# Requests for raw weights placed with the low that frees their buffer, v's weight sums requested with the last low, and another order of products in the latent opening

## The chip, the core and the metric

The kernel is one program on one core of a Trainium2 chip. Five engines run their own instruction streams: TensorE (PE in the profile; its weight loads are PEld), VectorE (DVE), ScalarE (ACT), GpSimd (POOL) and SyncE (SP, which here only issues transfers). The metric is device time in microseconds of one execution; lower is better. Values are the median of several runs.

## What is computed

Two layers over 512 latent and 256 context tokens of width 1024, float32. Each layer is a half-step SwiGLU FFN, a token mixer and a second half-step FFN, each with its input modulated by shift and scale, its output gated, and closed by a layer norm. Layer 0 mixes with a chunked gMLP, layer 1 with attention. Only the latent tokens are returned, so the last FFN runs over the latent tokens alone.

```python
def swiglu(h, w_in, w_out):
    g, u = jnp.split(h @ w_in, 2, axis=-1)
    return (jax.nn.silu(g) * u) @ w_out

def ffn_sublayer(x, shift, scale, gate, w_in, w_out, ln_g, ln_b):
    y = swiglu(modulate(x, shift, scale), w_in, w_out)
    return layer_norm(ALPHA * x + 0.5 * gate * y, ln_g, ln_b)

def gmlp_mix(h, w_in, sgu_g, sgu_b, w_s, b_s, w_out):
    u, v = jnp.split(jax.nn.gelu(h @ w_in, approximate=False), 2, axis=-1)
    v = layer_norm(v, sgu_g, sgu_b)
    ...
    return (u * v.reshape(b_, t_, GMLP_HALF)) @ w_out
```

## The kernel before

**Weights.** All weights come from HBM in pieces of 128x512 float32, 256 KB, called raws. `weight_order` writes out by hand the one order in which the whole kernel needs them. `load_raw` requests the next of that list on SP's queue as long as fewer than six raw buffers are out; `drop(n)` says that n buffers are given back and so requests n more; `take` hands over the oldest raw. SP's stream is pinned to program order, and a request there waits at the head of the queue until the last reader of its buffer is done.

**Units.** PE multiplies in a reduced float32 format, so a weight is used as a high part and a low part. `unit_of` makes a unit (w, eight buffers) of a raw or of a sum: ACT casts the high part (`hi`), and DVE subtracts to give the low part, the low. `split_later` (L175) issues the cast at once and puts the low on a list, `lows`; `flush` (L180) issues the lows. Each `slot`, the work between two groups of matmuls, begins with a flush, and then `pump` makes the next units, up to eight ahead of PE. So a low is issued one slot after its cast, unless `weights` needs it earlier.

**Strassen products.** The in-projections use a variant of Strassen's scheme: of four weight quarters (g1, g2, u1, u2) and four quarters of the activations, seven products are formed. `units` (L326) makes the seven units of a tile, with sums of raws on DVE: L348 and L351 make the first sums, L359 subtracts u1 from g1 in place, L367 makes the last. The units of u1 and u2 are split from the raw itself, so their raw buffer is free when their low has been made. Where a unit is a sum in a buffer of its own, the raws are free when that sum has been made.

**gmlp_v** (L1481) forms v, the second half of the gMLP's in-projection, in three pairs of 512 columns. For its sums of u1 and u2, `load_sums` (L429) loads the one raw into a buffer (acc, of which there are four) from SP's queue and lets a transfer of POOL's queue add the other to it on the way. `units_of_pair` (L437) subtracts a raw from the sum (`held`, on DVE), and later splits the sum itself: the lows of these four units (`s1`) are the last readers of acc. `load_sums` is called at the start of the stage, after the step T1 of the first pair, and after T1 of the second.

**The gMLP loop** (`gmlp`, L1623) then forms u in 12 pairs of 128 columns; in each it fetches pieces of v on SP's queue and fetches modulation weights (mraw), also on SP's queue, which DVE reduces into an accumulator.

**The latent opening.** The last FFN is `ffn_latent` (L1421). It starts while the layer norm ahead of it still runs: its first ten products are `open_pair(p, half)` in the order of `OPEN_LAT`, where p is a pair of column blocks and half is the part of the input that it multiplies. The first part of the activations (`comb`) is ready earlier than the second; between products, PE also transposes normalised rows, which ACT copies out (`pieces`, z). Its remaining weights are made by `units_of_tiles` (L385), and `out_proj_latent` follows. The weights of `OPEN_LAT` are requested in the same order (L229).

The steps of the prediction touch: `drop` and `take` (L308 to L312), `split_later`, `unit_of`, `units`, `units_of_tiles`, `load_sums`, `units_of_pair`, `gmlp_v` and `OPEN_LAT` (L64).

Of the kernel before, what the change touches and what calls it, by code (L numbers as in the profile page):

```python
# [7 lines left out]
F32 = mybir.dt.float32  # L8
F32R = mybir.dt.float32r
AF = mybir.ActivationFunctionType  # L10
ALU = mybir.AluOpType
# [49 lines left out]
KEPT_MIX, READ_BACK_MIX = 2, 10  # L61
KEPT_LAT, READ_BACK_LAT = 6, 9
OPENED_PAIRS = 5
OPEN_LAT = [(0, 0), (1, 0), (0, 1), (2, 0), (1, 1), (3, 0), (2, 1), (4, 0), (3, 1), (4, 1)]  # L64

PARTS = (0, 0), (0, 1), (1, 0)

# [31 lines left out]
class Backbone:  # L99
# [72 lines left out]
        self.dve.tensor_tensor(lo, src, hi.bitcast(F32), ALU.subtract)  # L172
        return i.ins

    def split_later(self, hi, lo, src, key=None):  # L175

        self.act.copy(hi, src)  # L177
        self.lows.append((key, lambda: self.dve.tensor_tensor(lo, src, hi.bitcast(F32), ALU.subtract)))  # L178

    def flush(self):  # L180
        lows, self.lows = self.lows, []
# [30 lines left out]
    def weight_order(self):  # L212
# [6 lines left out]
        def ffn(l, s, strassen=True, kernel_start=False):  # L219
# [3 lines left out]
            def cut(o, f, half):  # L223
                return wi[:, 4 * half : 4 * half + 4, o + f * P : o + f * P + P]

            start = FIRST_OPEN + SECOND_OPEN if kernel_start else OPEN
            if not strassen:
                two = lambda o, p, half: [cut(o, f, half) for f in (2 * p, 2 * p + 1)]
                jobs.append(("u", [s for p, half in OPEN_LAT for s in two(0, p, half)]))  # L229
                for p in range(FF // 2):  # L230
# [76 lines left out]

    def take(self):  # L308
        self.load_raw()
        return self.wraw.pop(0)  # L310

    def drop(self, n):  # L312
# [3 lines left out]
    def sums(self):  # L316
        return self.main.tile([P, 512], F32, tag="sums", bufs=2, name="sums")

    def unit_of(self, src):
        w = self.main.tile([P, 2, 512], F32R, tag="w", bufs=W_BUFS, name="w")  # L320
        self.split_later(w[:, 0], w[:, 1], src, w)
        if not self.slots:
            self.flush()
        return w

    def units(self, jobs):  # L326
        dve, w = self.dve, None
        for kind, srcs in jobs:
            if kind == "u":
                for _ in srcs:  # L330
                    w = self.unit_of(self.take())
                    self.drop(1)
                    yield w
                continue
            if kind in "vw":
                yield from self.units_of_pair(kind == "w")
                continue
            if kind in "RS":
                yield from self.units_of_tiles(kind == "R")
                continue  # L340
            g1 = self.take()
            if kind == "s":
                yield self.unit_of(g1)
            u1, u2 = self.take(), self.take()
            if any(key is w for key, _ in self.lows):
                self.flush()
            s1, s2 = self.sums(), self.sums()
            dve.tensor_tensor(s1, u1, u2, ALU.add)  # L348
            if kind == "s":
                yield self.unit_of(s1)  # L350
            dve.tensor_tensor(s2, s1, g1, ALU.subtract)  # L351
            second = self.unit_of(s2)
            yield second
            if kind == "r":
                yield self.unit_of(s1)
            else:
                g2 = self.take()
                yield self.unit_of(g2)
            dve.tensor_tensor(u1, g1, u1, ALU.subtract)  # L359
            w = self.unit_of(u1)  # L360
            self.drop(2)
            yield w
            if kind == "r":
                g2 = self.take()
            if any(key is second for key, _ in self.lows):
                self.flush()
            dve.tensor_tensor(s2, g2, s2, ALU.subtract)  # L367
            w = self.unit_of(s2)
            self.drop(1)
            yield w  # L370
            w = self.unit_of(u2)
            self.drop(1)
            yield w

    def load_tile_sums(self):

# [8 lines left out]
    def units_of_tiles(self, opened):  # L385

        sub = lambda out, a, b: self.dve.tensor_tensor(out, a, b, ALU.subtract)
        self.load_tile_sums()
        g1 = [self.take() for _ in range(2)]
        if not opened:  # L390
            for g in g1:
                yield self.unit_of(g)
        s1 = [self.tile_sums.pop(0) for _ in range(2)]
        if not opened:
            for s in s1:
                yield self.unit_of(s)
        s2, second = [], []
        for g, s in zip(g1, s1):
            s2.append(self.sums())
            sub(s2[-1], s, g)  # L400
            second.append(self.unit_of(s2[-1]))
            yield second[-1]
        if opened:
            for s in s1:
                yield self.unit_of(s)
        else:
            g2 = [self.take() for _ in range(2)]
            for g in g2:
                yield self.unit_of(g)
        for g in g1:  # L410
            u1 = self.take()
            sub(u1, g, u1)
            w = self.unit_of(u1)
            self.drop(2)
            yield w
        for x in range(2):
            g = self.take() if opened else g2[x]
            if any(key is second[x] for key, _ in self.lows):
                self.flush()
            sub(s2[x], g, s2[x])  # L420
            w = self.unit_of(s2[x])
            self.drop(1)
            yield w
        for _ in range(2):
            w = self.unit_of(self.take())
            self.drop(1)
            yield w

    def load_sums(self):  # L429

        self.u_sums = [self.acc() for _ in range(4)]
        u1, u2 = self.pair_sums.pop(0)
        for k in range(4):
            self.sp.dma_start(self.u_sums[k], u1[k])
            self.pool.dma_start(self.u_sums[k], u2[k], accum_op=ALU.add)

    def units_of_pair(self, first):  # L437

        def of_raw():
            for _ in range(4):  # L440
                w = self.unit_of(self.take())
                self.drop(1)
                yield w

        held = self.main.tile([P, 4, 512], F32, tag="gate", bufs=1, name="held")
        s1, units = self.u_sums, []
        for k in range(4):
            g1 = self.take()
            self.dve.tensor_tensor(held[:, k], s1[k], g1, ALU.subtract)
            units.append(self.unit_of(held[:, k]))  # L450
            self.drop(1)
            yield units[k]
        if first:
            yield from of_raw()
        else:
            for k in range(4):
                yield self.unit_of(s1[k])
        for k in range(4):
            g1, u1 = self.take(), self.take()
            self.dve.tensor_tensor(u1, g1, u1, ALU.subtract)  # L460
            w = self.unit_of(u1)
            self.drop(2)
            yield w
        if first:
            for k in range(4):
                yield self.unit_of(s1[k])
            yield from of_raw()
        for k in range(4):
            g2 = self.take()
            if any(key is units[k] for key, _ in self.lows):  # L470
                self.flush()
            self.dve.tensor_tensor(held[:, k], g2, held[:, k], ALU.subtract)
            w = self.unit_of(held[:, k])
            self.drop(1)
            yield w
        if not first:
            yield from of_raw()
# [943 lines left out]
    def ffn_latent(self, l, i, nblocks, end, prev):  # L1421
# [3 lines left out]
        self.combining = self.combine_latent()  # L1425
        for n, (p, half) in enumerate(OPEN_LAT):
            self.open_pair(p, half, self.seed if n == len(OPEN_LAT) - 2 else None)
        acts = Acts(self, FF, LAT, KEPT_LAT, READ_BACK_LAT, f"act{l}{i}_")
# [52 lines left out]
    def gmlp_v(self, room, spill, vst):  # L1481
# [61 lines left out]
        def zs():  # L1543
            return [self.zplace() for _ in range(HALF)]

        def ms():
            return [
                self.main.tile([P, 512], F32, tag="mraw", bufs=MRAW_BUFS, name="p5") for _ in range(HALF)
            ]

        def keep(p):
            return lambda t, ps: act.copy(p[t], ps)
# [10 lines left out]
        def kept_and_seeded(p5, u2):  # L1563

            def evacuate(t, ps):
                act.copy(p5[t], ps)
                act.copy(ps, u2[t])

            return evacuate
# [19 lines left out]
        u2 = zs()  # L1589
# [3 lines left out]
        step(1, "T3", True, keep(u3))  # L1593
        p5 = ms()
        step(0, "T1", False, kept_and_seeded(p5, u2))
        self.load_sums()

        def fourth(t, ps):
            out(1, t, ps)
# [6 lines left out]
        for x, a, seed in ((1, 2, p2), (0, 4, None)):  # L1606
            y = 1 - x
            u2 = zs()
            step(x, "T2", True, keep(u2))
            p5 = ms()  # L1610
            step(y, "T1", False, kept_and_seeded(p5, u2))
            if seed:
                self.load_sums()
            step(x, "T3", True, lambda t, ps, a=a, p5=p5: summed(a + 1, HALF + t, ps, p5[t]))
            step(y, "B22", True, both(a, p5, seed))
            step(x, "T4", True, lambda t, ps, a=a: out(a + 1, t, ps))
# [938 lines left out]
```

## Time and profile before

| | |
|---|---|
| median of 3 runs | 2761.05 us (2759.3 to 2762.8) |
| the profiled execution | 2765.46 us, its span 2763.5 us |
| mean granted clock of TensorE | 0.996 |
| PE busy | 2713.8 us, 98% of the span |
| DVE, ACT, POOL busy | 2135.2, 1375.4, 675.7 us |
| SP's queue (q1) | 343.00 MB, 40.5% of the 16 DMA engines' time |
| POOL's queue (q0) | 122.42 MB, 15.5% |

The stages that the change touches most lie at 559 to 739 us (gmlp_v), 740 to 954 (the gMLP loop) and 2400 to 2439 (the latent opening). In a timeline, each row gives start, duration, engine, line, operation, what it writes and reads, and how many there were in a row; in brackets stands the idle time of that engine ahead of it and what ended the idle time. L94 is the line of the helper that pins an instruction, so instructions are told apart by their tiles. "SPq" and "POOLq" stand for transfers issued on the queues of SP and POOL.

### The profile page before, as it was taken

The numbers are of one execution on the slowest core, as the hardware profiler recorded it, in microseconds if no ns is written. First come the engines' busy times: TensorE is split into PE (matmuls) and PEld (weight loads), VectorE is DVE, ScalarE is ACT, GpSimd is POOL, SyncE is SP. The second block draws the span as 40 slices with busy tenths as digits, with TensorE's granted clock in tenths as the row PEclk, the third lists the DMA queues.
The fourth block names the chain that finished last, engine by engine and source line by source line (L and its number), as shares of the span: only waits on it lengthen the run. The fifth ranks groups of instructions, "written<-read, shape, count | busy, mean of one in ns | idle before, by whom it ended". The sixth has DMA issues, their size and how long they took to land.

```text
span 2763.5 us, 42802 instructions
## 1 busy us (share of the span) xinstructions
PE 2713.8 (98%) x14930; PEld 2479.1 (90%) x14930; DVE 2135.2 (77%) x3724; ACT 1375.4 (50%) x2755; POOL 675.7 (24%) x829
## 2 busy tenths in 40 slices
PE   7999999999999999999999999999999999999998
PEld 5999987888899988899998889999988888899987
DVE  6878878576779977687888658788786598788865
ACT  6644433375666632564444237444432666665532
POOL 1003245312113344100324130024253121112221
PEclk9999999999999999999999999999999999999999
DMA  7445466367665684444446534454595424489772
GB/s 236 134 141 143 145 217 223 110 198 229 196 200 182 198 274 127 133 146 149 138 144 220 175 108 137 141 155 138 170 309 168 144 78 75 135 212 237 196 230 87
DMA packets 442896, 468.15 MB, mean 169 GB/s; under 512 B 30840, under 2 KB 323128, under 8 KB 442680
## 3 DMA queue, kind: packets, MB, share of 16 engines
q1 hardware_dynamic: 393592, 343.00, 40.5%
q0 software_dynamic: 49088, 122.42, 15.5%
q8 instruction: 117, 1.92, 0.3%
q14 instruction: 99, 0.81, 0.1%
HBM read 401.75 MB, written 65.77 MB: 169 GB/s over the span
## 4 chain that ended last, share of the span: by engine, by line
PE 74%; DVE 7%; issue 6%; ACT 5%; DMA 4%; POOL 3%; SPq 0%; DVEq 0%; ACTq 0%; POOLq 0%
PE ps L94 74%; POOL acc L544 2%; DVE w L94 2%; DMA raw<-in_ffn_w_in_dram 1%; ACT w L94 1%; PE pp L94 1%; ACT h L765 1%; DMA raw<-in_w_mod_dram 1%; DVE q L94 1%; ACT z L2453 0%; ACT w L177 0%; DVE z L94 0%; DMA acc<-in_gmlp_w_in_dram 0%; DMA q<-act 0%; POOL rs L208 0%
## 5 line engine op out<-in xcount | busy, mean ns | idle before, releaser
L94 PE MATMUL ps<-comb,w 128*128 128x384 f32 (+1 forms) x8400 | 1379.3, 324 | 14.0 <-ACT pieces L94 3.7
L94 PEld LDWEIGHTS ps<-comb,w 128*128 128x128 f32 x8400 | 1360.2, 189 | 21.3 <-ACT pieces L94 4.3
L94 PE MATMUL ps<-w,acts 128*128 128x512 f32 (+1 forms) x3792 | 861.6, 388 | 1.6 <-DVE q L94 0.8
L94 PEld LDWEIGHTS ps<-w,acts 128*128 128x128 f32 x3792 | 706.9, 188 | 148.5 <-ACT acts L94 1.2
L94 DVE TENSOR_TENSOR w<-raw,w 128x512 fp32r<-128x512 f32 x651 | 453.2, 703 | 258.8 <-ACT w L94 256.4
L94 ACT CAST w<-raw 128x512 fp32r<-128x512 f32 x651 | 399.4, 622 | 496.3 <-PE ps L94 395.1
L544 POOL PARTITION_ALL_REDUCE acc<-acc x224 | 294.9, 1388 | 260.2 <-DVE acc L94 231.8
L94 DVE SCALAR_TENSOR_TENSOR acc<-mraw,cs,acc 128x512 f32<-128x512 f32 x392 | 285.2, 761 | 16.1 <-DMA mraw<-in_w_mod_dram 15.7
L94 ACT COPY q<-ps 128x384 f32<-128x384 f32 (+1 forms) x248 | 122.1, 495 | 257.7 <-PE ps L94 257.0
L94 POOL DMA_DIRECT2D act<-stage x92 | 59.4, 716 | 779.8 <-DVE stage L94 733.7
L94 DVE TENSOR_TENSOR w<-sums,w 128x512 fp32r<-128x512 f32 x278 | 191.4, 697 | 52.6 <-ACT w L94 51.5
L94 POOL DMA_DIRECT2D q<-act x240 | 135.9, 621 | 338.1 <-DVE acts L94 197.3
L94 ACT CAST w<-sums 128x512 fp32r<-128x512 f32 x278 | 171.6, 621 | 62.2 <-DVE sums L94 30.7
L94 DVE TENSOR_TENSOR acts<-q,acts 128x384 fp32r<-128x384 f32 (+2 forms) x278 | 152.3, 587 | 32.5 <-ACT acts L94 32.5
L94 PE MATMUL ps<-w,comb 128*128 128x512 f32 x756 | 173.8, 390 | 3.3 <-ACT ps L94 2.9
L94 PEld LDWEIGHTS ps<-w,comb 128*128 128x128 f32 x756 | 141.3, 188 | 34.4 <-ACT ps L94 3.8
L94 ACT CAST acts<-q 128x384 fp32r<-128x384 f32 (+2 forms) x278 | 132.0, 512 | 72.1 <-DMA q<-act 54.3
L208 POOL TENSOR_TENSOR rs<-ve,mhalf 128x1 f32<-128x1 f32 (+3 forms) x47 | 38.2, 812 | 264.6 <-DVE ve L205 161.1
L94 ACT ACTIVATE q<-q 128x384 f32<-128x384 f32 (+1 forms) x94 | 51.3, 553 | 87.2 <-DVE q L94 87.2
L348 DVE TENSOR_TENSOR sums<-raw 128x512 f32<-128x512 f32 x78 | 55.1, 707 | 41.0 <-DMA raw<-in_gmlp_w_in_dram 25.4
L94 PE MATMUL ps<-w,h 128*128 128x512 f32 x336 | 78.2, 391 | 0.0
L178 DVE TENSOR_TENSOR w<-raw,w 128x512 fp32r<-128x512 f32 x93 | 61.7, 687 | 18.8 <-ACT w L177 18.4
(201 smaller groups left out, 2459.4 us busy)
## 6 DMA issues: line engine op xcount, KB each, us to landing
raw<-in_ffn_w_in_dram SPq DMA_DIRECT2D x420, 256.0 KB, 3.4
mraw<-in_w_mod_dram SPq DMA_DIRECT2D x256, 256.0 KB, 3.0
raw<-in_ffn_w_out_dram SPq DMA_DIRECT2D x176, 256.0 KB, 2.9
q<-act POOLq DMA_DIRECT2D x224, 192.0 KB, 4.1
raw<-in_gmlp_w_in_dram SPq DMA_DIRECT2D x132, 256.0 KB, 3.3
act<-stage POOLq DMA_DIRECT2D x76, 384.0 KB, 3.2
zhat<-z POOLq DMA_DIRECT2D x26, 512.0 KB, 3.0
raw<-in_gmlp_w_out_dram SPq DMA_DIRECT2D x48, 256.0 KB, 4.6
```

The source lines that it names most:

```text
L94: return self.tc.keep_in_program_order(f(*args, **kwargs))
L178: self.lows.append((key, lambda: self.dve.tensor_tensor(lo, src, hi.bitcast(F32), ALU.subtract)))
L208: self.last_rstd = self.nc.gpsimd.tensor_tensor(rs, ve, self.mhalf[:, 0:1].to_broadcast([P, n]), ALU.pow).ins
L348: dve.tensor_tensor(s1, u1, u2, ALU.add)
L544: nc.gpsimd.partition_all_reduce(part, part, P, bass_isa.ReduceOp.add)
L765: self.act.activation(h32[:, kk], ps[:, s], AF.Identity, bias=bi, scale=sc)
```

## The change

Three things. (1) The request that takes the place of a raw enters SP's queue when the low that reads this raw is issued, not when its cast is issued: `drop` becomes an argument of `unit_of` and is done in the function that issues the low. Where a unit of u1 gave two raws back, the one that only its subtraction reads is given back at once, and the other with the low. `take` issues the waiting lows if no raw is requested. (2) `load_sums` of v is called by the last low of `s1` (through the argument `then`), no longer after T1; the call at the start of the stage stays. (3) `OPEN_LAT` has (2, 0) third and (0, 1) fourth. What is computed is the same.

```diff
-OPEN_LAT = [(0, 0), (1, 0), (0, 1), (2, 0), (1, 1), (3, 0), (2, 1), (4, 0), (3, 1), (4, 1)]
+OPEN_LAT = [(0, 0), (1, 0), (2, 0), (0, 1), (1, 1), (3, 0), (2, 1), (4, 0), (3, 1), (4, 1)]

-    def split_later(self, hi, lo, src, key=None):
+    def split_later(self, hi, lo, src, key=None, drop=0, then=None):
         self.act.copy(hi, src)
-        self.lows.append((key, lambda: self.dve.tensor_tensor(lo, src, hi.bitcast(F32), ALU.subtract)))
+
+        def low():
+            self.dve.tensor_tensor(lo, src, hi.bitcast(F32), ALU.subtract)
+            if drop:
+                self.drop(drop)
+            if then:
+                then()
+
+        self.lows.append((key, low))

     def take(self):
         self.load_raw()
+        if not self.wraw:
+            self.flush()
         return self.wraw.pop(0)

# units: a raw that is split itself ("u" jobs; the same in units_of_tiles and units_of_pair)
-                    w = self.unit_of(self.take())
-                    self.drop(1)
-                    yield w
+                    yield self.unit_of(self.take(), 1)

# units: g1 less u1 (the same in units_of_tiles and units_of_pair)
             dve.tensor_tensor(u1, g1, u1, ALU.subtract)
-            w = self.unit_of(u1)
-            self.drop(2)
-            yield w
+            self.drop(1)
+            yield self.unit_of(u1, 1)

# units: u2
-            w = self.unit_of(u2)
-            self.drop(1)
-            yield w
+            yield self.unit_of(u2, 1)

     def load_sums(self):
+        if not self.pair_sums:
+            return
...
# units_of_pair, both places
             for k in range(4):
-                yield self.unit_of(s1[k])
+                yield self.unit_of(s1[k], 0, self.load_sums if k == 3 else None)

# gmlp_v
         step(0, "T1", False, kept_and_seeded(p5, u2))
-        self.load_sums()
...
             step(y, "T1", False, kept_and_seeded(p5, u2))
-            if seed:
-                self.load_sums()
```

More of the change, by code (lines that the diff above doesn't have):

```diff
@@ L317, in sums, with unit_of @@
         return self.main.tile([P, 512], F32, tag="sums", bufs=2, name="sums")
-    def unit_of(self, src):
+    def unit_of(self, src, drop=0, then=None):
         w = self.main.tile([P, 2, 512], F32R, tag="w", bufs=W_BUFS, name="w")
-        self.split_later(w[:, 0], w[:, 1], src, w)
+        self.split_later(w[:, 0], w[:, 1], src, w, drop, then)
         if not self.slots:
@@ L412, in units_of_tiles @@
             sub(u1, g, u1)
-            w = self.unit_of(u1)
-            self.drop(2)
-            yield w
+            self.drop(1)
+            yield self.unit_of(u1, 1)
         for x in range(2):
@@ L424, in units_of_tiles @@
         for _ in range(2):
-            w = self.unit_of(self.take())
-            self.drop(1)
-            yield w
+            yield self.unit_of(self.take(), 1)
     def load_sums(self):
+        if not self.pair_sums:
+            return
         self.u_sums = [self.acc() for _ in range(4)]
@@ L440, in of_raw @@
             for _ in range(4):
-                w = self.unit_of(self.take())
-                self.drop(1)
-                yield w
+                yield self.unit_of(self.take(), 1)
         held = self.main.tile([P, 4, 512], F32, tag="gate", bufs=1, name="held")
@@ L460, in units_of_pair @@
             self.dve.tensor_tensor(u1, g1, u1, ALU.subtract)
-            w = self.unit_of(u1)
-            self.drop(2)
-            yield w
+            self.drop(1)
+            yield self.unit_of(u1, 1)
         if first:
             for k in range(4):
-                yield self.unit_of(s1[k])
+                yield self.unit_of(s1[k], 0, self.load_sums if k == 3 else None)
             yield from of_raw()
```

## The prediction

> **What bounds the kernel now.** I read the page first, for the busy time of each engine.
>
> ```profile
> span 2763.5 us, 42802 instructions
> PE 2713.8 (98%) x14930; PEld 2479.1 (90%) x14930; DVE 2135.2 (77%) x3724; ACT 1375.4 (50%) x2755; POOL 675.7 (24%) x829
> ```
>
> TensorE (PE) works for 2713.8 of 2763.5 us. The change adds and removes no matmul, so its whole field is the difference, 49.7 us. It can shorten the kernel only where PE now stands still, or runs at a lower clock, for something that the change brings earlier. It can lengthen it anywhere. So the second view is the waits of PE: what PE waited for, the sum in us, how often, the longest.
>
> ```profile
> PE ps L94 <- ACT w L177: 7.5, 6, 2.6
> PE ps L94 <- DVE q L94: 3.9, 3, 2.0
> PE ps L94 <- ACT pieces L94: 3.7, 3, 2.8
> PE ps L94 <- ACT ps L94: 2.9, 2, 1.7
> ```
>
> The largest row belongs to weights that are split at L177 by `split`, not by `split_later`; the change does not touch that. The other three rows hold 10.5 us together, and each of their long waits turns out below to be in a stage that the change touches. The third view is what SyncE's queue (SPq), which issues the weight loads in program order, waits for; the fourth is the row of the page for the sums of two raw weights, with the idle time of VectorE (DVE) ahead of them as the last numbers.
>
> ```profile
> SPq L94 <- DVE w L94: 994.9, 494, 17.3
> SPq L94 <- DVE acc L94: 437.6, 204, 7.3
> L348 DVE TENSOR_TENSOR sums<-raw 128x512 f32<-128x512 f32 x78 | 55.1, 707 | 41.0 <-DMA raw<-in_gmlp_w_in_dram 25.4
> ```
>
> SPq already stands for 994.9 us at 494 requests that wait for a low (`DVE w`) to free a raw buffer. So before the change the request is in the queue early and waits at its head for that low. After it, the request is put there together with the low. The moment of the transfer is the low's end in both. What differs is only what stands ahead of and behind the waiting request in the same queue.
>
> **Part one: requests with the low.** What is removed is a wait at the queue's head; what is added is nothing; what is moved is one position in SPq for a request whose low is held back to the next `flush`. In the program every slot begins with `flush`, and in nearly every stage nothing else is put on SPq between the slot's pump and that flush, so the order on SPq stays as it is: in the strassen in-projections the units whose buffers are freed fall in slots without a fill, in the gMLP loop the fetch of v and the modulation load (mraw) are put there after the flush. It does change in the latent out-projection, in the last tile of an FFN, and in the `S` pairs of the latent FFN, where a fetch or an mraw now goes ahead of raws that wait for lows. There PE has no wait in the list above, and the units are made seven or eight ahead of use. POOL's queue holds none of these requests. The extra `flush` in `take` acts only if no raw is requested at all, which six buffers prevent. So I take 0. Its bounds come from the gMLP loop, where PE's waits for `DVE q` are.
>
> ```profile
> 841.98 6.44 SPq L94 DMA_DIRECT2D raw<-in_gmlp_w_in_dram  x3
> 846.73 0.69 DVE L348 TENSOR_TENSOR sums<-raw 128x512 f32<-128x512 f32 x1 [2.96 <-DMA raw<-in_gmlp_w_in_dram]
> 849.15 6.53 PE L94 MATMUL ps<-comb,w 128*128 128x384 f32 x36 [1.98 <-DVE q L94]
> 886.41 3.91 PE L94 MATMUL ps<-comb,w 128*128 128x384 f32 x21 [1.12 <-DVE q L94]
> ```
>
> Three raws are issued from 841.98; DVE, in order, stands 2.96 us before the sum at 846.73 because the raw has not landed; the evacuations of PSUM behind it are late, and PE idles 1.98 us at 849.15. The same happens with 1.12 us at 886.41. If the first raw came 3 us earlier, 1.98 + 1.12 = 3.1 us would go: that is the upper bound of a gain. But the first of those raws is requested right after the subtraction at L359, before the change and after it (the `drop(2)` became a `drop(1)` at that point and one with the low), so I see no reason for an earlier issue. The bound of a loss is among the rivals.
>
> **Part two: v's weight sums.** `load_sums` issues four loads on SPq and four accumulating loads on POOL, each of the latter after its partner has landed. The change requests them as soon as the last low that reads the previous sums has been issued, instead of after the T1 step. In the timeline (start, duration, engine, instruction, and in brackets the idle time ahead and what ended it):
>
> ```profile
> 623.98 0.68 DVE L94 TENSOR_TENSOR w<-acc,w 128x512 fp32r<-128x512 f32 x1
> 633.73 1.85 SPq L94 DMA_DIRECT2D acc<-in_gmlp_w_in_dram  x4
> 642.08 0.69 DVE L94 TENSOR_TENSOR held<-acc,raw 128x512 f32<-128x512 f32 x1 [3.62 <-DMA acc<-in_gmlp_w_in_dram]
> 648.98 0.69 DVE L94 TENSOR_TENSOR held<-acc,raw 128x512 f32<-128x512 f32 x1 [1.46 <-DMA acc<-in_gmlp_w_in_dram]
> 654.65 5.53 PE L94 MATMUL ps<-w,comb 128*128 128x512 f32 x23 [1.72 <-ACT ps L94]
> 660.17 0.69 DVE L94 TENSOR_TENSOR w<-acc,w 128x512 fp32r<-128x512 f32 x1
> 674.68 1.85 SPq L94 DMA_DIRECT2D acc<-in_gmlp_w_in_dram  x4
> 686.00 0.69 DVE L94 TENSOR_TENSOR held<-acc,raw 128x512 f32<-128x512 f32 x1 [3.04 <-issue]
> 696.96 3.24 PE L94 MATMUL ps<-w,comb 128*128 128x512 f32 x13 [1.19 <-ACT ps L94]
> ```
>
> The last low of the first sums ends at 624.66, the loads start at 633.73: they can be 633.73 - 624.66 = 9.1 us earlier. For the second the low ends at 660.86 and the loads start at 674.68: 13.8 us earlier. DVE waits for the sums 3.62 and 1.46 us in the first pair and 3.04 in the second (the profile says "issue" there, but the sum is read at 686.00, 11.3 us after the first issue, as 642.08 is 8.3 after its own). Earlier by 9.1 and 13.8 us, these waits of at most 3.62 us go entirely. What is late next is nothing that I find: the raws for `held` are there, and in the rest of this stage PE has no wait. The two PE idles behind DVE's delay are 1.72 + 1.19 = 2.91 us. I take -2.9.
>
> What could eat it: 2 MB more are in flight from 661 on, when raws for the u1 units are requested (the first row is the SPq stretch, the second and third are medians from issue to landing in 640 to 674 and 674 to 690).
>
> ```profile
> 662.09 12.54 SPq L94 DMA_DIRECT2D raw<-in_gmlp_w_in_dram  x11
> raw<-in_gmlp_w_in_dram SPq DMA_DIRECT2D x14, 256.0 KB, 3.1
> raw<-in_gmlp_w_in_dram SPq DMA_DIRECT2D x8, 256.0 KB, 6.4
> 667.43 0.69 DVE L94 TENSOR_TENSOR raw<-raw 128x512 f32<-128x512 f32 x1
> ```
>
> Beside the loads a raw takes 6.4 instead of 3.1 us, 3.3 more. A raw requested at 662.09 would land at 668.5, and DVE reads one at 667.43: some 1.1 us late, once or twice per pair, and then PE's slack in PSUM decides. Price 0 to 2.9 (all of the gain). I take 0, since a DVE wait of 3.62 us cost PE only 1.72, so 1.1 us should cost little.
>
> **Part three: the order of products in the latent opening.** `OPEN_LAT` takes (2, 0) as its third product and (0, 1) as its fourth. The cover of the transposes and normalisation is what is moved; the DMAs of units 5 to 8 are the same loads in another order.
>
> ```profile
> 2404.25 3.11 PE L94 MATMUL ps<-comb,w 128*128 128x256 f32 x24
> 2410.18 4.59 PE L94 MATMUL ps<-comb,w 128*128 128x256 f32 x24 [2.82 <-ACT pieces L94]
> 2414.22 0.62 ACT L94 CAST w<-raw 128x512 fp32r<-128x512 f32 x1
> 2414.86 1.28 ACT L94 ACT_TABLE_LOAD   x1
> 2416.15 0.60 ACT L94 ACTIVATE pieces<-ps 128x512 f32<-128x512 f32 x1
> 2419.39 1.18 ACT L94 CAST w<-raw 128x512 fp32r<-128x512 f32 x2
> 850.00:853.00 3.00, 3.00 (x19) 3.00 (x18) 3.00 (x8) 3.00 (x9) 0.00 (x0) 1.00 0.70 191
> 2408.00:2410.00 2.00, 0.00 (x0) 0.00 (x0) 0.16 (x1) 1.58 (x2) 0.23 (x2) 1.00 0.94 274
> 2410.00:2412.00 2.00, 1.82 (x12) 1.82 (x13) 0.42 (x1) 2.00 (x7) 0.53 (x1) 0.83 1.12 320
> 2412.00:2415.00 3.00, 3.00 (x17) 3.00 (x17) 2.26 (x5) 2.70 (x7) 1.35 (x1) 0.54 0.41 156
> 2415.00:2418.00 3.00, 3.00 (x28) 3.00 (x27) 0.65 (x2) 2.99 (x6) 1.28 (x1) 1.00 0.97 155
> 2420.00:2424.00 4.00, 3.89 (x33) 3.89 (x33) 4.00 (x8) 4.00 (x10) 0.00 (x0) 1.00 0.45 132
> ```
>
> The windows (the first is behind the gMLP's idle, for comparison) give stretch, length, then PE, PEld, DVE, ACT and POOL busy, then the granted clock. The third product needs the same `comb` half as the first two and its weights; (0, 1) needs pieces that ScalarE (ACT) copies late, and PE idles 2.82 us. Then the granted clock falls to 0.83 and 0.54, and the 24 matmuls take 4.59 us where the product before took 3.11: 1.48 us more. With (2, 0) in that place the idle goes and probably the slow clock: 2.82 + 1.48 = 4.3 us at most.
>
> But ACT is full from 2410 on (2.00 of 2, 2.70 of 3, 2.99 of 3, 4.00 of 4), and the fifth product's second half needs unit 10, cast by ACT at 2419.39. The same ACT work has to be done in another order. What comes ahead of unit 10's cast now and goes behind it is the table load and the silu of (0, 1), 1.28 + 0.60 = 1.9 us; what goes ahead instead is one more copy of about 0.6 us. So unit 10 can be 1.3 us earlier, and of that more is lost at unit 12, for which ACT has had the same list to do. So the gain is between 0 and 1.3, and I take 0.7. If ACT's cover were gone it would be 4.3.
>
> PE then idles later: the fourth product ends near 2413.9, unit 9 is cast by 2414.84 (0.9 us), its product takes about 1.1, and unit 10 comes at 2418.1 (2.3 us; estimates from these rows). The trace has an idle of 2.82 us followed by a clock near 0.5, and one of 1.98 (at 849.15) followed by a clock of 1.00; 2.3 lies between, so the 1.48 us may be paid again: -0.7 could become +0.8. This end stays in the range. The Trainium skill, "TensorE: Matmul & The Clock Gate", Part 1, says that the clock halves after an idle window of about 3.4 us, free-running; by that rule neither 2.3 nor 2.82 us would do it, and the sum would stay at -3.6. The trace disagrees for 2.82 us, where the clock did fall, so I keep the dearer end.
>
> **The sum.** 0 - 2.9 - 0.7 = -3.6 us. The profiled execution takes 2765.46 us with a span of 2763.5; it would become 2761.9 with a span of 2759.9. It lies 4.4 us over the median of the runs, 2761.05, so the median becomes 2757.4. About 0.2%, 5.5 us, is what a measurement of this kernel can tell from no change.
>
> **Rivals.** First, as summed (2757.4): for it speaks that each term is a wait in PE's own list.
>
> Second, more than that: ACT does not hold the latent opening, or the gMLP's raws do come earlier. The first alone gives -2.9 - 4.3 = -7.2, so 2753.9; with 3.1 from the gMLP it is -10.3, so 2750.8. For it speaks that both idles stand in the trace next to code that the change touches; against it ACT's full windows and the unmoved request at L359.
>
> Third, nothing: v's raws become late by what the sums gain, and ACT keeps the opening. The program does the same transfers at the same lows. 2761.
>
> Fourth, slower: in the gMLP loop, the raw requested with u1's low falls behind the fetch of v and the mraw that waits for DVE's accumulator (437.6 us of such waits on SPq). Each pair would then show the stall that two of them show now, (1.98 + 1.12) / 2 = 1.55 us; with ten more of the twelve pairs that is 15.5 us, less 3.6: +11.9, so 2773. It decides once the landing is later than DVE's sum by about 3 us, as at 846.73. Against it: by the program the flush precedes the fetch.
>
> **How the numbers follow.** As summed 0.46, more 0.30, nothing 0.17, slower 0.07. The likeliest gives 2757.4; its own range is 2755 to 2760. The range for 8 in 10 runs from 2752, inside the second case, to 2762.5, which holds the third and the clock's dearer end; left out are the fourth case and the far end of the second, about 0.15. Faster by over 0.2% is the second case, 0.30; slower the fourth, 0.07; within 0.2% the rest, 0.63.
>
> **What would show it.** The `acc` loads issued near 625 and 661; no DVE idle before `held<-acc`; PE's two waits for `ACT ps` gone. The third latent product starting near 2407.4 without idle and at clock 1.00, and the wait near 2418 on an ACT cast. SPq's 494 waits for `DVE w` fewer, but the landing of raws unmoved. I am wrong if PE's waits in the gMLP loop change by more than 2 us, if new PE waits stand between 662 and 680, or if the product after the latent opening starts over 2 us earlier against the one before it.

## The result and the profile after

The changed kernel takes 2757.08 us (median of 20 runs, 2754.39 to 2761.54); the kernel before, measured beside it, 2762.54 us (20 runs, 2758.19 to 2765.51). The ratio is 0.9982, with a 95% interval of 0.9975 to 0.9989: 3 to 7 us less, about 5. The forecast was 2757.4 us, 3.6 less. The profiled execution took 2757.46 us; that of the kernel before took 2765.46, so these two differ by 8.0 us, 2.5 more than the medians, and a part of what their two profiles tell apart is chance.

The page's head:

```profile
span 2755.7 us, 42815 instructions
PE 2712.2 (98%) x14930; PEld 2477.9 (90%) x14930; DVE 2137.1 (78%) x3724; ACT 1379.9 (50%) x2755; POOL 678.1 (25%) x829
```

PE's field, span less busy time, went from 49.7 to 43.5 us. What PE waits for (sum, times, longest; L177 is `split`, which the change leaves alone):

```profile
PE ps L94 <- ACT w L177: 6.6, 7, 2.9
PE ps L94 <- ACT w L94: 3.6, 3, 2.4
PE ps L94 <- DVE q L94: 0.2, 1, 0.2
```

The waits for `ACT pieces` (3.7) and `ACT ps` (2.9) no longer stand there, and that for `DVE q` fell from 3.9 to 0.2. A new row has come: 3.6 us for casts of weights. SyncE's queue:

```profile
SPq L94 <- DVE w L94: 1002.6, 511, 17.3
```

Against 494 requests before, 511 now wait for a low. So placing a request together with the low did not take waits from the head of the queue, as the prediction had it; there are a few more, and their sum is 1002.6 us where it was 994.9.

In v's stage (start, duration, instruction, idle time ahead), with the medians of landing in 640 to 674 us behind it:

```profile
621.29 2.97 SPq L94 DMA_DIRECT2D acc<-in_gmlp_w_in_dram  x4
649.34 5.11 SPq L94 DMA_DIRECT2D acc<-in_gmlp_w_in_dram  x4
642.21 0.69 DVE L94 TENSOR_TENSOR held<-acc,raw 128x512 f32<-128x512 f32 x1
678.66 0.68 DVE L94 TENSOR_TENSOR held<-acc,raw 128x512 f32<-128x512 f32 x1
639.78 65.44 PE L94 MATMUL ps<-w,comb 128*128 128x512 f32 x288
raw<-in_gmlp_w_in_dram SPq DMA_DIRECT2D x15, 256.0 KB, 9.2
acc<-in_gmlp_w_in_dram SPq DMA_DIRECT2D x4, 256.0 KB, 3.3
```

The loads go out at 621.29 and 649.34 (633.73 and 674.68 before), the subtractions have no idle time ahead of them, and PE runs from 639.78 for 65 us without one gap. The raws pay for it, 9.2 us to land where it was 3.1, and PE does not wait for them. The second load is earlier than the working had it: each of the four waits only for the low of its own buffer, not for the last of them, and DVE makes these lows sooner (the first at 648.63, at 655.40 before), since it is no longer late.

The latent opening:

```profile
2395.80 5.99 PE L94 MATMUL ps<-comb,w 128*128 128x256 f32 x48
2402.42 3.11 PE L94 MATMUL ps<-comb,w 128*128 128x256 f32 x24
2406.45 1.69 PE L94 MATMUL ps<-comb,w 128*128 128x256 f32 x12 [0.92 <-ACT w L94]
2410.58 11.70 PE L94 MATMUL ps<-comb,w 128*128 128x256 f32 x83 [2.44 <-ACT w L94]
2410.60:2412.60 2.00, 2.00 (x15) 2.00 (x16) 1.95 (x4) 1.97 (x3) 0.00 (x0) 0.85 0.90 117
2412.60:2414.60 2.00, 2.00 (x11) 2.00 (x11) 1.10 (x2) 2.00 (x5) 0.00 (x0) 0.50 0.87 250
```

Second and third product run through as one block of 48; then PE idles 0.92 and 2.44 us before the two halves of the fifth, and the granted clock (third number from the right) falls to 0.50 again. The 2.82 us did not go; an idle of 3.4 us in all stands two products later.

**Where the time went.** The same 14930 matmuls run in the same order in every kernel here, so each trace can be cut at the same matmuls. The table gives the us between them, named by their time in the kernel before. "again" is the unchanged kernel profiled once more; e1 and so on are the experiments below; e6 and e7, where the opening is made in another way, are left out.

```
stretch        before  again |   e1     e2     e3     e4     e5    e11 |    e8     e9 | after    e10
20-60           39.88  38.47 |  38.08  38.16  39.23  38.04  40.49  36.11 |  36.62  37.63 |  38.27  38.44
60-415         355.01 355.97 | 355.06 355.45 355.44 355.02 355.03 357.09 | 356.13 355.53 | 355.52 355.39
645-665         19.94  19.51 |  19.95  17.91  19.98  17.91  17.91  17.91 |  17.91  17.91 |  17.91  17.91
690-705         14.85  13.69 |  13.37  13.37  13.80  13.37  13.37  13.37 |  13.37  13.37 |  13.37  13.37
740-965        225.06 224.37 | 220.96 221.58 222.27 221.39 221.92 221.29 | 221.36 221.25 | 221.23 220.62
1165-1215       49.89  49.83 |  49.21  49.79  49.69  49.22  49.69  49.47 |  49.88  49.24 |  49.33  49.22
1670-1720       50.09  50.24 |  49.96  50.27  49.92  49.83  50.38  50.07 |  50.63  49.73 |  49.83  49.77
2400-2424       24.03  24.02 |  24.87  24.03  24.35  24.78  23.81  23.17 |  24.08  24.15 |  24.44  23.19
2440-2520       80.05  81.01 |  79.03  81.29  81.07  81.37  82.09  81.64 |  81.20  80.48 |  80.24  81.19
```

Three rows differ between executions whatever the kernel: 20-60 by 4 us, 60-415 and 2440-2520 by 2 to 3. The largest of these is nearly what the whole change is worth, so a step is judged by its own stretch, and the times carry only the sum. In the row 740-965, counted matmul by matmul over all fourteen profiles (e6 and e7 too), the differences sit mostly in two places. At 849 us stands the one long stall: 2.1 and 2.0 us more than in the shortest in the two profiles of the unchanged kernel, 0.14 in e3 and none in the others (the second unchanged profile lost 1.7 us more behind it). At 886 us it is 0 to 1.3 us in the seven with the tiles' old requests (0.8 on the mean) and 0 to 0.6 in the seven with the new ones (0.2).

### The profile page after: what moved, and what is told of

It reads as the page before. It is cut to its first block, busy times and chain, and to the rows that moved or that the text cites. A ratio compares the mean times of both kernels' runs of the same rounds, so it can differ in the third digit from the quotient of the medians.

```text
span 2755.7 us, 42815 instructions
## 1 busy us (share of the span) xinstructions
PE 2712.2 (98%) x14930; PEld 2477.9 (90%) x14930; DVE 2137.1 (78%) x3724; ACT 1379.9 (50%) x2755; POOL 678.1 (25%) x829
## 4 chain that ended last, share of the span: by engine, by line
PE 79%; DVE 5%; issue 5%; ACT 4%; POOL 3%; DMA 3%; SPq 0%; DVEq 0%; POOLq 0%; ACTq 0%
PE ps L94 78%; POOL acc L545 2%; DMA raw<-in_ffn_w_in_dram 1%; DVE w L94 1%; PE pp L94 1%; DMA raw<-in_w_mod_dram 1%; ACT h L766 1%; ACT z L2451 1%; ACT w L177 0%; DVE acc L94 0%; DVE z L94 0%; ACT w L94 0%; POOL rs L216 0%; DMA q<-act 0%; DVE w L180 0%
```

## The experiments

All ratios are to the kernel before, timed beside each run, with their 95% intervals.

**The kernel before, again.** No edit.

> The kernel before, unchanged, as a control. Every theory: a ratio of 1.000, PE idles of about 1.7 and 1.2 us in v's second and third pair, and 2.8 us in the latent opening. Theory one (the gMLP's idles of 0.39, 1.98 and 1.12 us belong to the order of the requests): they come again within 0.5 us each. Rival (they come from how long a raw takes to land, which differs from one execution to the next): their sum between 740 and 960 us differs from 3.5 by more than 1 us.

Ratio 0.9994 (0.9985 to 1.0002). Two of PE's idles in this profile, one in v and one in the gMLP loop:

```profile
655.01 50.26 PE L94 MATMUL ps<-w,comb 128*128 128x512 f32 x219 [1.29 <-ACT ps L94]
847.51 8.10 PE L94 MATMUL ps<-comb,w 128*128 128x384 f32 x36 [1.79 <-DVE q L94]
```

In v's third pair no gap of PE shows now (50.26 us in one row), where 1.19 us stood. In the gMLP loop one idle stands where there were three, 1.8 us where it was 3.5: the rival is right that they come and go. What an idle costs differs too: behind this one of 1.79 us the granted clock fell (0.50 from 849.5 to 851.5), and the 36 matmuls took 8.10 us, where the same 36 took 6.53 at 1.00 behind the 1.98 us of the first profile. The opening's 2.82 us came again to the hundredth. A part of what one profile of before seemed to offer was chance.

**Part one alone (e1).**

```diff
-OPEN_LAT = [(0, 0), (1, 0), (2, 0), (0, 1), ...
+OPEN_LAT = [(0, 0), (1, 0), (0, 1), (2, 0), ...
...
-                yield self.unit_of(s1[k], 0, self.load_sums if k == 3 else None)
+                yield self.unit_of(s1[k])
...
         step(0, "T1", False, kept_and_seeded(p5, u2))
+        self.load_sums()
```

(against the changed kernel; the second call of `load_sums` is put back likewise)

> Part one alone (requests with the low), with v's loads and the opening's order as before. The prediction's theory: no change in time, within 1 us, v's idles of 1.7 and 1.2 us and the opening's 2.8 us as before. Rival (the order of the requests took away the gMLP's idles): 3 to 4 us faster, no PE idle over 0.5 us between 740 and 960 us.

Ratio 0.9992 (0.9984 to 1.0001), some 2 us less, not clear of no change. By its stretches the gMLP loop is 220.96 us, with no idle of PE over 0.5 us as the rival had it, and the two FFN starts are 49.21 and 49.96 instead of 49.8 and 50.2. At the FFN starts nothing is changed but the place of the requests, and the first lies clear of every profile that has the tiles' old requests (49.47 to 49.89), so part one is not worth nothing; the second lies within theirs (49.92 to 50.63). v's idle of 1.7 us stays, as expected; the one of 1.2 did not come here either.

**Part two alone (e2).**

```diff
+        def low():
+            self.dve.tensor_tensor(lo, src, hi.bitcast(F32), ALU.subtract)
+            if then:
+                then()
...
-                yield self.unit_of(s1[k])
+                yield self.unit_of(s1[k], self.load_sums if k == 3 else None)
...
         step(0, "T1", False, kept_and_seeded(p5, u2))
-        self.load_sums()
```

> Part two alone (v's weight sums requested with the last low). The prediction's theory: 2.9 to 3.5 us faster, no DVE idle over 1 us before the subtraction from acc in v's second and third pair, no PE idle over 0.5 us there. Rival (the raws behind the loads become late and give it back): idles of PE of 1 us or more between 660 and 690 us, and under 1.5 us faster.

Ratio 0.9992 (0.9984 to 1.0001). The two stretches in v are 17.91 and 13.37, as in the changed kernel:

```profile
639.64 65.67 PE L94 MATMUL ps<-w,comb 128*128 128x512 f32 x289
raw<-in_gmlp_w_in_dram SPq DMA_DIRECT2D x15, 256.0 KB, 8.8
```

No gap of PE in 65 us, though the raws take 8.8 us to land. The rival, late raws that give the gain back, falls. Against the four executions without part two (before, again, e1, e3) the two stretches gain 2.0, 1.6, 2.1 and 2.0 in the first place and 1.5, 0.3, 0.0 and 0.4 in the second: 2.5 us on the mean.

**Part three alone (e3), and parts one and two without it (e4).**

```diff
-OPEN_LAT = [(0, 0), (1, 0), (0, 1), (2, 0), ...
+OPEN_LAT = [(0, 0), (1, 0), (2, 0), (0, 1), ...
```

> Part three alone (the other order of the latent opening). The prediction's theory: 0.7 us faster, the 2.8 us of idle gone from the third product. What the changed kernel's trace suggests instead: no change within 0.5 us, with idles of 0.9 and 2.4 us in the fifth product in place of 2.8, and a granted clock near 0.5 for some 3 us behind them again.

> Parts one and two, with the opening's order of before. If part three is worth nothing (what its run alone shows): the time of the changed kernel within 0.5 us, that is 5 us less than before. The prediction's theory (0.7 us from part three): 0.7 us slower than the changed kernel. In the gMLP loop (740 to 960 us), if the requests with the low take away its idles, as in both kernels so far that had them: no PE idle over 0.5 us; if it is chance: idles of 0.5 to 2 us may come.

e3: 0.9997 (0.9988 to 1.0006), with idles of 0.91 and 2.38 us and the clock at 0.50 behind them, as expected. e4: 0.9981 (0.9972 to 0.9990), as the changed kernel; 0.7 us more or less is not to be told with intervals of 2.5 us either way. In e4's gMLP loop the one idle over 0.5 us is 0.81, for `ACT q`, at its end. With the old order the stretch of the opening took 24.03, 24.02, 24.87, 24.03 and 24.78 us, with the new one 24.35, 23.81, 23.17, 24.08, 24.15, 24.44 and 23.19: 24.35 against 23.88 on the mean, a gain of 0.5 with a spread as large.

The spread is in the main the clock: with the new order the stretch takes 24.1 to 24.4 us in the four profiles where it fell, on the mean 24.3 as with the old order, and 23.2 to 23.8 in the three where it did not. In the changed kernel's second profile (e10) the same idles are there:

```profile
2405.89 1.70 PE L94 MATMUL ps<-comb,w 128*128 128x256 f32 x12 [0.91 <-ACT w L94]
2409.68 3.13 PE L94 MATMUL ps<-comb,w 128*128 128x256 f32 x24 [2.10 <-ACT w L94]
2409.70:2411.70 2.00, 2.00 (x17) 2.00 (x18) 1.95 (x4) 1.97 (x3) 0.00 (x0) 1.00 0.84 107
2411.70:2413.70 2.00, 1.67 (x14) 1.47 (x13) 1.10 (x2) 2.00 (x5) 0.00 (x0) 1.00 0.87 254
```

Here 24 matmuls take 3.13 us at a clock of 1.00; in the first profile 11 matmuls filled 2 us at 0.50.

**Parts two and three without part one (e5, and once more as e11).** e2's edit with e3's.

> Parts two and three, without part one. The prediction's theory (part one is worth nothing): the time of the changed kernel, 5 us less than before. Rival (part one is worth what its run alone gave, 2 us): 2 us slower than the changed kernel, so some 3 us less than before, with a third idle of 0.3 to 0.5 us at the start of each of the two FFNs near 1202 and 1710 us again, and PE idles of 0.5 to 2 us in the gMLP loop.

> Parts two and three without part one, once more. By the stretches of its trace it should be 2 to 3 us faster than the kernel before (4 us in v's two places, less what the FFN starts, the gMLP loop and the latent FFN vary). If it shows no gain again, something that the traces of the stretches do not hold makes it slower.

Ratios 1.0001 (0.9992 to 1.0010) and 0.9996 (0.9988 to 1.0005). In both, v's stretches are at 17.91 and 13.37, so 2.5 us are gained there, and yet the times show little of it. As the rival had it, e5's FFN starts take 49.69 and 50.38 us and an idle of 0.94 us stands in its gMLP loop, but e5 lost more than the rival's 2 us. In e5's profile 20-60 and 2440-2520 are the longest of all (40.49 and 82.09); in e11's, 60-415 is (357.09). Beside e11 on the same chip the changed kernel (e10) is at 0.9979 (0.9970 to 0.9987), with medians of 2755.45 against 2759.53 us: part one makes some 4 us there, and some 2 where it stands alone, with intervals of some 2.5 us either way on each of these ratios.

**The changed kernel with the tiles' requests as before (e8).**

```diff
             dve.tensor_tensor(u1, g1, u1, ALU.subtract)
-            self.drop(1)
-            yield self.unit_of(u1, 1)
+            w = self.unit_of(u1)
+            self.drop(2)
+            yield w
...
-            yield self.unit_of(u2, 1)
+            w = self.unit_of(u2)
+            self.drop(1)
+            yield w
```

> The changed kernel with the requests for u1 and u2 of the strassen tiles (in units alone) placed as before; everything else of the change stays. Theory now (what part one gives comes from these requests: DVE's order at the two FFN starts, and the gMLP loop): the matmuls of 1165 to 1215 us and of 1670 to 1720 us (times of the kernel before) take 49.7 and 50.2 us again, not 49.3 and 49.8, and those of 740 to 965 us take 222 us or more, not 221.2; 2 to 3 us slower than the changed kernel. Rival (it comes from elsewhere or from chance): the three stretches as in the changed kernel.

> The changed kernel itself, once more, to compare with on the same chip. Every theory: 5 us less than before, 17.9, 13.4 and 221.2 us in the stretches 645 to 665, 690 to 705 and 740 to 965 us.

e8: 0.9988 (0.9979 to 0.9996), median 2758.20 us; e10, on the same chip: 0.9979 (0.9970 to 0.9987), median 2755.45, its stretches 17.91, 13.37 and 220.62. So e8 is 2.7 us slower, as expected, though the intervals overlap. The FFN starts are back at 49.88 and 50.63 us (e10: 49.22 and 49.77), as expected. The gMLP loop is not: 221.36 us, with the tiles' old requests in it, where 222 or more was expected. That half of the theory falls.

What happens at an FFN start, in the rows of the kernel before (L359 takes u1 from g1; ACT's cast of it stands ahead of the copy that frees PE's bank):

```profile
1208.01 0.69 DVE L94 TENSOR_TENSOR w<-sums,w 128x512 fp32r<-128x512 f32 x1
1208.61 0.69 DVE L359 TENSOR_TENSOR raw<-raw 128x512 f32<-128x512 f32 x1
1209.34 0.62 ACT L94 CAST w<-raw 128x512 fp32r<-128x512 f32 x1 [1.69 <-DVE raw L359]
1209.86 0.47 ACT L94 COPY q<-ps 128x384 f32<-128x384 f32 x1
1210.39 2.90 PE L94 MATMUL ps<-comb,w 128*128 128x384 f32 x15 [0.32 <-ACT q L94]
```

and of the changed kernel (the subtraction is L367 there):

```profile
1202.91 0.69 DVE L367 TENSOR_TENSOR raw<-raw 128x512 f32<-128x512 f32 x1
1203.52 0.69 DVE L94 TENSOR_TENSOR w<-sums,w 128x512 fp32r<-128x512 f32 x1
1203.62 0.62 ACT L94 CAST w<-raw 128x512 fp32r<-128x512 f32 x1
1185.79 27.47 PE L94 MATMUL ps<-comb,w 128*128 128x384 f32 x157
```

and of e8:

```profile
1199.62 0.68 DVE L94 TENSOR_TENSOR w<-sums,w 128x512 fp32r<-128x512 f32 x1
1200.22 0.68 DVE L367 TENSOR_TENSOR raw<-raw 128x512 f32<-128x512 f32 x1
1200.94 0.62 ACT L94 CAST w<-raw 128x512 fp32r<-128x512 f32 x1 [1.68 <-DVE raw L367]
1201.99 11.19 PE L94 MATMUL ps<-comb,w 128*128 128x384 f32 x63 [0.32 <-ACT q L94]
```

In `units`, DVE's sums of raws (L348 to L367 before) are not pinned to program order. With the request for u1's neighbour put right behind the subtraction, DVE has the subtraction ahead of the lows instead of behind them, ACT's cast does not wait 1.69 us, the copy behind it is not late, and PE does not idle. So the gain is one of DVE's order, not of a transfer. That the place of the request is what moved the subtraction is inferred from e8, where only these requests differ; how it moves it was not followed.

**One request of the gMLP loop put back (e9).**

```diff
             bs, r = bias[:, g % 2], bias[:, 2 + g % 2]
+            self.flush()
             self.sp.dma_start(bs, io["gmlp_b_s"][0, g].unsqueeze(0).to_broadcast([P, P]))
```

> The changed kernel with one request put back: the fetch of the gMLP's bias row (S) for the second group again behind the raw that waits for a low, by issuing the lows ahead of it. If this place in the queue makes the gMLP loop shorter: 740 to 965 us (times of the kernel before) takes 222 us or more again and the kernel is 1 to 2 us slower than the changed one, with the FFN starts unchanged at 49.3 and 49.8 us. Rival (the loop's length comes from how long raws take to land): 221 to 221.5 us, no difference.

0.9978 (0.9969 to 0.9987), and the loop takes 221.25 us: this place in the queue is worth nothing. With e8, and with e2, e5 and e11, which have nothing of part one, it says that the loop is short also with the old order of its requests. The three profiles of the table with neither part one nor part two have 222.3 to 225.1 us there, the nine with one or both 220.6 to 221.9. Why stays open: no order of requests that was put back explains it, and no run tells chance from some state in which v's stage leaves the engines. The long stall at 849 us is missing in e3 too, which has neither part.

**More units ahead in the opening (e6), and that with the old order (e7).**

```diff
 LEAD = 3
+LEAD_LAT = 6
...
         if self.combining is not None:
-            self.pump(max(0, min(n, LEAD - len(self.wready))))
+            lead = LEAD_LAT if self.part_cols == LAT else LEAD
+            self.pump(max(0, min(n, lead - len(self.wready))))
```

> The changed kernel, with up to six units ready, not three, while the latent opening's parts are made, so that units 9 and 10 are cast in the idle time of ACT that ends near 2400 us. If the opening is held by the casts behind ACT's other work: the fifth product's idles of 0.9 and 2.4 us go, the granted clock stays at 1.00, and the time is 3 to 5 us less than the changed kernel's. Rival (ACT is full, and what goes ahead only moves the wait): the same idle in sum, 3 us or more, elsewhere between 2400 and 2425 us, and the same time within 0.7 us.

> The same with the opening's order of before. If the third product waits for its transposed input (pieces) and not for a cast: an idle near 2.8 us stays before the third product, whatever is ready, and the clock falls behind it, so that the time is 2 us or more above that of the kernel with more units and the new order. Rival (the order makes no difference): the same time within 0.7 us.

e6: 0.9975 (0.9966 to 0.9985), median 2755.96 us. e7: 0.9976 (0.9966 to 0.9986), 2756.92 us. In e6 (the helper's line is L95 there):

```profile
2405.09 11.95 PE L95 MATMUL ps<-comb,w 128*128 128x256 f32 x96 [0.53 <-ACT pieces L95]
2417.48 3.13 PE L95 MATMUL ps<-comb,w 128*128 128x256 f32 x24 [0.43 <-ACT pieces L95]
2422.78 7.45 PE L95 MATMUL ps<-comb,w 128*128 128x256 f32 x60 [2.17 <-ACT q L95]
2408.00:2412.00 4.00, 4.00 (x35) 4.00 (x35) 2.76 (x5) 3.98 (x9) 0.00 (x0) 1.00 1.33 223
```

The waits for casts are gone and PE idles 0.53 + 0.43 + 2.17 = 3.1 us elsewhere, against 0.92 + 2.44 = 3.4 in the changed kernel, while ACT is busy 3.98 of 4 us. That is the rival: ACT is full, and what goes ahead moves the wait. The clock did stay at 1.00 in e6. Its stretch of 2400-2424 is 19.86 us only because the longest wait now lies behind it: from the second product to the matmul at 2445 us of before, e6 takes 39.93 us, e10, where the clock was spared as well, 40.04, and the first profile of the changed kernel 41.28. e7 keeps 2.82 us before its third product and a fallen clock behind it (0.60 and 0.55 in the 4 us after), as expected, but not the 2 us or more that this was to cost: it is 1.0 us behind e6. Both ratios lie 0.0006 to 0.0007 below the changed kernel's, within the intervals: no version here is clearly faster than the changed one.

## Why the prediction was right, point by point

**v's sums, -2.9: right.** The waits of DVE went, PE's gaps went, nothing came late after them, and the raws' slower landing cost PE nothing. The second idle (1.19 us) was taken from one execution and is 0 to 1.5 in four, so the term is 2.5 on the mean, by four executions without part two; that the same waits go in e2, which has part two alone, shows the cause.

**The latent opening, -0.7: the mechanism right, the size within the noise.** The idles that were to come, 0.9 and 2.3 us, came as 0.92 and 2.44 (0.91 and 2.10 in the second profile), and ACT is what holds it. Unit 10 was to come 1.3 us earlier; its matmuls start 15.9 us behind the second product's in before, again and e2 (16.8 and 16.7 in e1 and e4, where the clock stayed down longer), and 14.5 to 15.1 with the new order, 0.8 to 1.4 us earlier. A small slip stands in the working: the first half of the fifth product takes 1.69 us (12 matmuls), not about 1.1. The clock's dearer end came in the first profile and not in the second, and where it came almost nothing is left of the gain. About 0.5 is left on the mean. That 2.3 us was put between a spared 1.98 and a punished 2.82 was no measure of the risk: 1.79 us was punished in the gMLP loop of the unchanged kernel, and 2.72 spared here.

**Requests with the low, 0: the step that failed**, though the range held it. The step was "what differs is only what stands ahead of and behind the waiting request in the same queue". The order on DVE differs too, where its instructions are not pinned, and at the two FFN starts that gives 0.5 + 0.4 us (49.75 to 49.24 and 50.23 to 49.82 on the mean over the table's kernels without and with the tiles' requests). The wait at the queue's head, which was to be removed, was not: 511 waits where fewer than 494 were named as a sign. The claim that the gMLP loop's order on SPq stays was wrong in one request, which e9 shows to cost nothing. PE's waits in that loop did change by more than the 2 us that were named as a sign of error: they came and went in the unchanged kernel as well.

One more place, in the latent FFN, has the mark of part one: the idle of 0.50 us at 2471.33, for `ACT pieces`. It is there, 0.1 to 1.1 us over the shortest, in all six profiles that request with the cast in this stage, and in none of the eight that request with the low (e8 among them, which puts back the tiles of `units` alone). How it went was not followed, and the row 2440-2520 as a whole, 81.2 us on the mean of the table's six without and 80.6 of the six with, gains less than it spreads.

**The sum.** 2.5 + 0.5 + 0.9 = 3.9 us by stretches. The timed difference is 5 (3 to 7). The gMLP loop, 223.9 us on the mean of three profiles without the change and 220.9 in the two of the changed kernel, would more than fill the gap, but its cause is open. Open too is why part one is worth more in the times (some 2 us alone, some 4 beside e11) than the 0.9 us that the FFN starts show: 0.6 at 886 us of the gMLP loop and 0.6 in the latent FFN would make it 2, but neither is clear of its spread. Why parts two and three alone show so little of v's gain is open as well.

**The number.** That 2757.08 us lies 0.3 from the forecast is luck. The kernel before took 1.5 us more than its first three runs had said, the gain was larger by about as much, and in the sum a term of 2.9 that was 2.5 stands beside one of 0 that was 0.9 or more.

**The rivals.** The one with more gain had the opening not held by ACT, but PE still waits there for casts of ACT (3.6 us), or the gMLP's raws earlier: the long idle there did go, but in kernels without part one too (e2, e3, e5, e11). The slower one had raws of the gMLP loop behind the mraw at every pair. No such stall came.

## What to carry to other kernels

A wait that one profile shows may be chance: profile the unchanged kernel twice, cut both traces at the same instructions, and count as gain only stretches that differ from both. Where an engine's order is left to the compiler, moving a request in one queue can reorder another engine, so compare the order of every engine, not only of the one edited. An idle in front of an engine that is already full, here ACT, came back a few microseconds later when it was moved.

## What the runs showed of the hardware

After PE idles of 0.9 and then 2.1 to 2.7 us, with 1.7 us of matmuls between, the granted clock fell to 0.50 in four profiles of seven with the new order (second idle 2.38, 2.44, 2.11, 2.32 us) and stayed at 1.00 in three (2.72, 2.10, 2.11). With the old order, after 2.82 us, it fell in all six profiles. The length of the idle does not decide it: 2.72 was spared, and of two of 2.11 one was and one was not. In the gMLP loop an idle of 1.79 us alone was enough in one execution of the kernel before, and one of 1.98 at the same matmul was spared in the other. The Trainium skill, "TensorE: Matmul & The Clock Gate", Part 1, has the clock halve after an idle window of about 3.4 us and calls this window free-running. A window that runs freely would fit what is seen, but no run here shows it; and page and traces differ in that idles of 1.79 to 2.82 us were enough.

In v's stage (640 to 674 us) a raw took a median of 9.2 us to land in the changed kernel, 8.8 in e2 and 8.1 in e4, where the second pair's eight loads of acc (2 MB) go out in that time, against 3.1 to 3.2 in before, again, e1 and e3, where they go out later (from 674.68 in before).
